# The last four experts as one group, and a scheduler that prices changes of array shape

## The chip, the cores and the metric

The kernel runs on one core of a Trainium2 chip. A core has TensorE (PE in the profile, its weight loads PEld), VectorE (DVE), ScalarE (ACT), GpSimd (POOL) and SyncE (SP), which here issues the DMAs. The metric is the device time of one execution in microseconds (us). A run's time is a little longer than the span of its trace, which goes from the first to the last instruction.

## The reference

Two transformer blocks over 256 tokens of width 1024, all in float32. The first has a modulated mixer (a spatial gating half, a convolution half) and a feed-forward part. The second has a pooling and a sparse attention mixer, an attention to a memory, and then a mixture of 32 experts, of which each token takes two of the eight in its group:

```python
g_sel = jnp.argmax(g_logits, axis=-1)
top_v, top_i = lax.top_k(e_in, TOP_K_EXPERTS)
top_w = jax.nn.softmax(top_v, axis=-1) * g_w
...
for g in range(N_GROUPS):
    a = jnp.einsum('nd,edf->nef', hf, w_gate[g])
    b = jnp.einsum('nd,edf->nef', hf, w_up[g])
    hid = jax.nn.silu(a) * b * gates[:, g, :, None]
    out = out + jnp.einsum('nef,efd->nd', hid, w_down[g])
return x + out
```

An expert has two matrices of 1024x256 (gate, up) and one of 256x1024 (down). All 32 make 96 loads of 1 MB, about half of the 212 MB that the kernel reads.

## The kernel before, in words

The weights lie in one stream in the order of `plan()` (line 217), in loads of 128 rows by 2048 numbers (1 MB). SBUF has 26 regions (`R0` to `R25`) of that size; most loads go to a region that has come free, in the stream's order, on SP's one queue. A DMA is issued when the region's last reader has run, and at most eight are under way.

`Recorder` records every operation with what it depends on, and `flush` (line 737) then orders them. `plan` (line 567) is a list scheduler: it steps through a time of its own in which an operation has the cost that `cost` (line 366) gives it, and picks on each engine the operation that can start first, by rank among those that can start together. `back` (line 700) makes new ranks from a finished order, and `PATH` (line 804) lists the rounds and the seeds of small changes to the ranks; the last order is issued. So each engine's instructions stand in one fixed order, and the engines wait for each other by semaphores. Nearly all instructions therefore have line 797, where `issue` emits them.

Where the scheduler sees TensorE idle for long enough, `plan` puts in products of a matrix of ones whose result nobody reads (`filler`, line 769, emitted at line 774). 92 such products stand in the order, 37 of them at the start.

Some matmuls use a part of the 128x128 array. A *column step* is four matmuls with 32 output rows each, side by side in four column tiles (`tile_position`), recorded as one operation (`rec.join`). `ada_pe` (line 1165) and `conv_pe` (line 1312) use them in the first block, the experts at lines 1939 to 1944 and 1969 to 1974. The value products of two attentions write 64 output rows, products of heads read 64 rows, and a few write or read 8.

`experts` (line 1914) goes over `GROUPS` (line 214): seven groups of four experts, and then two of two. The tokens of an expert stand in 32 slots. A group does this:

- `gather`: 16 products pick the tokens (`xg`).
- `gu`: eight column steps over the contraction (k), one load of 1 MB each, make gate and up in one bank `pg`. In a group of two a step has two column tiles, and one load holds two steps.
- `hid`: silu on ScalarE, a product on VectorE, two transposes.
- `dn`: four column steps with the down matrix make the experts' outputs `pd`, copied to `ye`. In a group of two, two experts and the two halves of the contraction take the four column tiles, and the halves are added in `combine` (`sw` is copied to both).
- `combine`: eight products by the weights `sw` add to the output `ac`.

The last group goes by quarters of 256 features in a fixed order (`rec.series`): `product`, `moved`, then `closing`, which combines, adds the residual and starts the output's DMA. A loop behind it takes tokens beyond 32 in an expert; in this input it doesn't run.

Of the kernel before, what the change touches and what calls it, by code (L numbers as in the profile page):

```python
# [15 lines left out]
KT = D // 128  # L16
# [78 lines left out]
def layout(v):  # L95
# [51 lines left out]
    for name, arg in PLAN:  # L147
# [17 lines left out]
        elif name == "fin":  # L165
            j = 256 * arg
            full(rowk(np.concatenate([fin[:, j:j + 256], fin[:, DF + j:DF + j + 256]], 1)))
        elif name == "fout":
            full(rowk(fout[512 * arg:512 * arg + 512]))
        elif name == "in2":  # L170
            pad = np.zeros((D, 56), np.float32)
            a = np.concatenate([win2[:, 2560:2632], pad, win2[:, 2048:2560], win2[:, 512:1536]],
                               1)[:, 512 * arg:512 * arg + 512]
            full(rowk(a) if arg == 0 else stat(a))
        elif name == "in2p":
            full(rowk(win2[:, 0:512]))
        elif name == "in2v":
            full(rowk(win2[:, 1536:2048]))
        elif name == "out2":
            full(rowk(wout2[512 * arg:512 * arg + 512]))  # L180
        elif name == "mk":
            full(rowk(wkv[:, 0:512]))
        elif name == "mv":
            full(rowk(wkv[:, 512:1024]))
        elif name == "wq":
            full(rowk(wq[:, 256 * arg:256 * arg + 256]))
        elif name == "wo":
            full(rowk(wo))
        elif name in ("gu", "dn"):
            (g_, s_), (q, e0, n) = arg, GROUPS[arg[0]]  # L190
            gg, e = q // 2, slice(4 * (q % 2) + e0, 4 * (q % 2) + e0 + n)
            if name == "gu":
                a = np.concatenate([eg[gg, e], eu[gg, e]], axis=-1).reshape(n, KT, 128, 512)
                full(a[:, 8 // n * s_:8 // n * (s_ + 1)].transpose(2, 1, 0, 3))
            elif n == 4:
                full(ed[gg, e].reshape(4, 2, 128, 2, 512)[:, s_].transpose(1, 2, 0, 3))
            else:
                full(ed[gg, e].reshape(2, 2, 128, 4, 256).transpose(2, 3, 1, 0, 4))
# [15 lines left out]
GROUPS = [(q, 0, 4) for q in range(7)] + [(7, 0, 2), (7, 2, 2)]  # L214


def plan():
# [13 lines left out]
    for g, (q, e0, n) in enumerate(GROUPS):  # L231
        p += [("gu", (g, s)) for s in range(n)] + [("dn", (g, s)) for s in range(n // 2)]
# [118 lines left out]
class Op:  # L351
    __slots__ = ("eng", "name", "args", "kw", "pos", "preds", "succs", "new", "bufs", "cost",
                 "set", "start", "end", "active", "calls")
# [12 lines left out]
def cost(eng, name, args, kw):  # L366
# [7 lines left out]
    if eng == "tensor":  # L374
# [4 lines left out]
        if "tile_position" in kw:  # L379
            return mv.free() * passes / 2.4e3 / 4 + 0.002  # L380
# [19 lines left out]
def activity(name, kw, c):  # L400
# [4 lines left out]
    return c if n >= 128 else c * n / 128  # L405

# [32 lines left out]
class Recorder:  # L439
# [3 lines left out]
    def __init__(self, nc, pools):  # L443
# [3 lines left out]
        self.hosts, self.series, self.joined = {}, None, None  # L447
# [39 lines left out]
    def record(self, eng, name, args, kw):  # L487
        if self.joined:
            op = self.joined[0]
            assert op.eng == eng  # L490
            c = cost(eng, name, args, kw)
# [16 lines left out]
        op.set = SETS.get(kw.get("func")) if eng == "scalar" else None  # L508
        self.ops.append(op)
# [57 lines left out]
    def plan(self, prio):  # L567
# [22 lines left out]
        table, oldest, order = None, 0, []  # L590
# [27 lines left out]
        while issued < n:  # L618
            best = None
            for e, rows in cands.items():  # L620
                pick = None
                for ready, op in rows:
# [10 lines left out]
                    rank = prio[op.pos] - (SWITCH if op.set and op.set != table else 0.0)  # L633
                    if pick is None or t < pick[0] or rank > pick[1]:
# [33 lines left out]
            if op.eng == "tensor":  # L668
                w = int(t / WINDOW)
# [131 lines left out]
SWITCH = 3.0  # L801
# [12 lines left out]
def _build(tc, a, out, ctx):  # L814
# [1093 lines left out]
    def combine(g, ye, sw, ac, ns=range(8)):  # L1908
        for j in ns:
            PE.matmul(out=ac[j], lhsT=ye[:, 128 * j:128 * j + 128], rhs=sw,  # L1910
                      start=(g == 0 and j % 2 == 0), stop=(g == len(GROUPS) - 1),
                      skip_group_check=True)

    def experts(ac, s8):
# [4 lines left out]
        for g, (q, e0, n) in enumerate(GROUPS):  # L1919
            if q % 2 == 0:  # L1920
                if s8 is None:
                    s8 = places(q)
                s8q, s8 = s8, None
                w8 = buf("U", 2, 8, CAP)
            if e0 == 0:
                gather(xg, s8q, q)
            if q % 2 == 0:
                for t in range(2):
                    V.tensor_tensor(out=w8[:, t], in0=s8q[:, t],
                                    in1=wt[:, t, 4 * q:4 * q + 8].unsqueeze(2).to_broadcast(  # L1930
                                        [128, 8, CAP]), op=ALU.mult)
            rows, first = slice(0, 32 * n), 4 * (q % 2) + e0
            pg = bank()
            k = 0
            for c in range(n):
                for reg in take("gu", (g, c), 2 if (g, c) == (len(GROUPS) - 1, 1) else 1):
                    w = view(reg, 0, 4 // n, n, 512)
                    for kk in range(4 // n):
                        with rec.join():
                            for e in range(n):  # L1940
                                o_ = 32 * (first + e)
                                PE.matmul(out=pg[32 * e:32 * e + 32], lhsT=xg[:, k, o_:o_ + 32],
                                          rhs=w[:, kk, e], start=(k == 0), stop=(k == KT - 1),
                                          tile_position=(0, 32 * e), skip_group_check=True)
                        k += 1
            S.activation(out=hid[rows], in_=pg[rows, 0:256], func=AF.Silu)
            V.tensor_tensor(out=hid[rows], in0=pg[rows, 256:512], in1=hid[rows], op=ALU.mult)
# [3 lines left out]
            for t in range(2):  # L1951
                PE.transpose(out=ps[rows, 128 * t:128 * t + 128],
                             in_=w8[:, t, first:first + n].rearrange("p e c -> p (e c)"),
                             identity=ident)
            for b in range(0, 128, 32 * n):
                S.copy(out=sw[b:b + 32 * n], in_=ps[rows, 0:T])
            ps = bank()
            for f in range(2):
                PE.transpose(out=ps[:, 128 * f:128 * f + 32 * n],
                             in_=hid[rows, 128 * f:128 * f + 128], identity=ident[rows, rows])  # L1960
            V.tensor_copy(out=hT.rearrange("p (f c) -> p f c", f=2)[:, :, rows],
                          in_=ps[:, 0:T].rearrange("p (f c) -> p f c", f=2)[:, :, rows])
            pd = [bank(), bank()]
            end = g == len(GROUPS) - 1
            if n == 4:
                for f in range(2):
                    for i, reg in enumerate(take("dn", (g, f))):
                        w = view(reg, 0, 4, 512)
                        with rec.join():
                            for e in range(4):  # L1970
                                PE.matmul(out=pd[i][32 * e:32 * e + 32],
                                          lhsT=hT[:, 128 * f + 32 * e:128 * f + 32 * e + 32],
                                          rhs=w[:, e], start=(f == 0), stop=(f == 1),
                                          tile_position=(0, 32 * e), skip_group_check=True)
# [4 lines left out]
            regs = take("dn", (g, 0), 2 if end else 1)  # L1979
            def product(i, m):  # L1980
                w = view(regs[i], 0, 2, 2, 2, T)
                with rec.join():
                    for f in range(2):
                        for e in range(2):
                            b = 64 * f + 32 * e
                            PE.matmul(out=pd[i][b:b + 32, T * m:T * m + T],
                                      lhsT=hT[:, 128 * f + 32 * e:128 * f + 32 * e + 32],
                                      rhs=w[:, m, f, e], start=True, stop=True,
                                      tile_position=(0, b), skip_group_check=True)

            def closing(i, m):
                j = 4 * i + 2 * m
                combine(g, ye, sw, ac, (j, j + 1))
                V.tensor_tensor(out=xt[:, j:j + 2], in0=ac.b[j // 2], in1=xt[:, j:j + 2],
                                op=ALU.add)
                SY.dma_start(out=out[:, j:j + 2], in_=xt[:, j:j + 2])

            def moved(i, m):
                c = 512 * i + T * m
                (V.tensor_copy if m else S.copy)(out=ye[:, c:c + T], in_=pd[i][:, T * m:T * m + T])  # L2000

            if end:
                steps = [(0, 0), (0, 1), (1, 0), (1, 1)]
                rec.series = {}
                for i, m in steps[:1]:
                    product(i, m)
                    moved(i, m)
                for n_, (i, m) in enumerate(steps):
                    if n_ + 1 < 4:
                        product(*steps[n_ + 1])  # L2010
                        moved(*steps[n_ + 1])
                    closing(i, m)
                rec.series = None
                continue
            for i in range(2):
                for m in range(2):
                    product(i, m)
            S.copy(out=ye[:, 0:512], in_=pd[0])
            V.tensor_copy(out=ye[:, 512:1024], in_=pd[1])
            last = (g, ye, sw, ac)  # L2020

# [4 lines left out]
    rounds = nc.values_load(nr.ap()[0:1, 0:1], min_val=1, max_val=8)  # L2026
    with tc.For_i(1, rounds, 1):
# [21 lines left out]
```

## Time and profile before

| | |
|---|---|
| median of three runs | 750.11 us (748.1 to 750.91) |
| profiled execution | 751.32 us, span 749.6 us |
| TensorE | 718.4 us busy (96%), 5466 records |
| VectorE, ScalarE | 418.1 us (56%), 311.3 us (42%) |
| stream's DMA queue | 211.55 MB, 72.9% of the 16 engines' time |
| granted TensorE clock | 0.987 on average |

A float32 product stands in the trace as two records. In rows of the timeline the third column from the engine is the operation with its tiles, then rows and columns of the array that it uses (128*32 is one column tile), then the output's shape; `xN` counts records, and what stands in brackets is idle time before it and what ended it. PE spans overlap a little, so that the start of the next row tells when an engine went on.

### The profile page before, as it was taken

How to read it: one execution, taken by the hardware profiler on the slowest of the kernel's cores; microseconds unless marked ns; L12 is line 12 of the kernel's file. 1: busy time of each engine (PE TensorE's matmuls, PEld its weight loads, DVE VectorE, ACT ScalarE, POOL GpSimd, SP SyncE). 2: the span in 40 equal slices, each digit the busy share in tenths (PEclk: the TensorE clock that was granted, in tenths of full speed). 3: DMA queues.
4: the chain of work that ended last, by engine and by line, in shares of the span. 5: the costliest groups of instructions: out<-in, count | busy, mean ns of one | idle time of the engine just before them, and what ended most of it. 6: DMA issues, size and time to landing. Idle time of an engine off the chain costs nothing.

```text
span 749.6 us, 13378 instructions
## 1 busy us (share of the span) xinstructions
PE 718.4 (96%) x5466; PEld 569.5 (76%) x5466; DVE 418.1 (56%) x876; ACT 311.3 (42%) x597; POOL 3.7 (0%) x18
## 2 busy tenths in 40 slices
PE   9999999999999999999999999999999999987894
PEld 9689676989999999999899768998844555442342
DVE  7679958694667577557787888466711221110002
ACT  6547647443544353446854547366521121110000
POOL 0010000000000000000000000000000000000000
PEclk9999999999999999999999999999999999999898
DMA  8997389996458668655621325973799999999981
GB/s 331 419 417 305 136 338 421 397 393 226 154 210 291 253 217 295 224 174 186 263 68 57 113 70 211 335 281 129 268 401 419 418 420 419 419 418 419 421 339 61
DMA packets 31603, 212.46 MB, mean 283 GB/s; under 512 B 3632, under 2 KB 4016, under 8 KB 7088
## 3 DMA queue, kind: packets, MB, share of 16 engines
q1 hardware_dynamic: 31536, 211.55, 72.9%
q8 instruction: 45, 0.74, 0.4%
q14 instruction: 22, 0.18, 0.1%
HBM read 210.48 MB, written 1.05 MB: 282 GB/s over the span
## 4 chain that ended last, share of the span: by engine, by line
PE 86%; DMA 7%; DVE 3%; ACT 1%; SPq 1%; issue 1%; ACTq 0%
PE B L797 85%; DMA R<-stream 7%; DVE R L797 2%; ACT R L797 1%; SPq L797 1%; PE B L774 1%; DVE s L797 0%; DVE U L797 0%; DVE gi L797 0%; DVE g L797 0%; DVE lgt L797 0%; DVE j L797 0%; DVE cond L797 0%; DVE i L797 0%; DVE ei L797 0%
## 5 line engine op out<-in xcount | busy, mean ns | idle before, releaser
L797 PE MATMUL B<-R,R 128*128 128x256 f32 (+4 forms) x4376 | 580.5, 366 | 12.3 <-DMA R<-stream 7.9
L797 PEld LDWEIGHTS B<-R,R 128*128 128x128 f32 (+2 forms) x4376 | 433.1, 169 | 86.7 <-issue 45.8
L797 ACT ACTIVATE R<-R 128x1024 fp32r<-128x1024 f32 (+4 forms) x268 | 187.9, 738 | 160.5 <-PE B L797 122.4
L797 DVE TENSOR_TENSOR R<-R,R 128x1024 fp32r<-128x1024 f32 (+3 forms) x214 | 192.0, 929 | 77.9 <-ACT R L797 73.8
L797 DVE TENSOR_TENSOR R<-B,R 128x256 f32<-128x256 f32 (+3 forms) x78 | 32.8, 440 | 72.3 <-ACT R L797 58.1
L797 ACT ACTIVATE R<-B 128x256 f32<-128x256 f32 (+4 forms) x82 | 27.6, 372 | 79.5 <-PE B L797 79.3
L797 ACT ACTIVATE R<-B,cv 128x128 f32<-128x128 f32 (+2 forms) x64 | 26.5, 423 | 79.3 <-PE B L797 79.0
L797 PEld LDWEIGHTS B<-U,R 128*128 128x128 f32 x256 | 34.0, 191 | 25.7 <-issue 19.3
L797 PE MATMUL B<-R 128*128 128x256 f32 (+4 forms) x200 | 49.0, 383 | 1.0 <-ACT R L797 1.0
L797 DVE COPY R<-B 128x256 f32<-128x256 f32 (+2 forms) x33 | 15.2, 464 | 59.1 <-PE B L797 59.0
L797 PEld LDWEIGHTS B<-R 128*128 128x128 f32 (+1 forms) x200 | 30.7, 193 | 21.0 <-issue 14.8
L797 ACT COPY R<-B 128x256 f32<-128x256 f32 (+3 forms) x35 | 13.9, 409 | 73.4 <-PE B L797 73.3
L797 DVE TENSOR_SCALAR R<-B,cv 128x128 f32<-128x128 f32 x32 | 11.2, 350 | 54.9 <-PE B L797 54.5
L797 PE MATMUL B<-U,R 128*128 128x128 f32 x256 | 40.2, 287 | 1.1 <-ACT R L797 0.7
L774 PEld LDWEIGHTS B<-ones 128*128 128x128 f32 x184 | 26.4, 217 | 13.9 <-issue 10.9
L774 PE MATMUL B<-ones 128*128 128x128 f32 x184 | 30.9, 313 | 1.5 <-POOL inv_h L797 1.4
L797 DVE SCALAR_TENSOR_TENSOR U<-R,ca,U 128x512 f32<-128x512 f32 x42 | 31.4, 748 | 0.6
L797 DVE SCALAR_TENSOR_TENSOR R<-R,cv,R 128x256 f32<-128x256 f32 (+1 forms) x54 | 25.2, 481 | 2.8 <-ACT R L797 1.7
L797 PE MATMUL B<-cst,R 128*128 128x128 f32 (+3 forms) x130 | 21.3, 255 | 4.3 <-DVE R L797 3.3
L797 PEld LDWEIGHTS B<-cst,R 128*128 128x128 f32 (+1 forms) x130 | 17.0, 163 | 8.7 <-DVE R L797 4.7
L797 ACT ACT_TABLE_LOAD x16 | 20.5, 1283 | 4.0 <-PE B L797 3.0
L797 DVE TENSOR_TENSOR R<-R 128x256 f32<-128x256 f32 x47 | 18.1, 421 | 2.1 <-ACT R L797 1.6
(123 smaller groups left out, 277.7 us busy)
## 6 DMA issues: line engine op xcount, KB each, us to landing
R<-stream SPq DMA_DIRECT2D x190, 1024.0 KB, 10.9
R<-stream SPq DMA_DIRECT2D x14, 512.0 KB, 12.0
R<-mt SPq DMA_DIRECT2D x2, 512.0 KB, 6.9
R<-xt SPq DMA_DIRECT2D x1, 1024.0 KB, 10.7
out_dram<-R SPq DMA_DIRECT2D x4, 256.0 KB, 2.5
cst<-cst SPq DMA_DIRECT2D x1, 533.0 KB, 18.7
R<-bands SPq DMA_DIRECT2D x1, 320.0 KB, 2.8
R<-cosin SPq DMA_DIRECT2D x1, 256.0 KB, 7.4
```

Source lines behind the costliest of these rows:

```text
L774: self.nc.tensor.matmul(out=self.pools["B"][k][:, 0:128], lhsT=ones, rhs=ones, start=True, stop=True)
L797: getattr(getattr(self.nc, op.eng), name)(*[real(v) for v in args], **{k: real(v) for k, v in kw.items()})
```

## The change

1. The last four experts are one group. `GROUPS` is 8, all groups have four experts, and each step four column tiles. In the last group the down matrix lies in the stream by quarters of the features, one load of 1 MB for each (the last two loads as two halves); a quarter is two column steps of 256 columns into a bank of its own, a copy to `ye`, two products of `combine`, the add and the output's DMA.
2. In the scheduler a column step of four costs what one of its matmuls costs (before, the sum of four quarters: nearly the same), a change of the array's shape costs time (`turn`), and an operation with another shape than the last loses half a microsecond of rank (`TURN`).
3. `PATH` is another list. No ones-matmul is put in behind the start of the experts (`rec.busy`).

```diff
-GROUPS = [(q, 0, 4) for q in range(7)] + [(7, 0, 2), (7, 2, 2)]
+GROUPS = 8
...
+def turn(a, b):
+
+    if not a or a == b:
+        return 0.0
+    c = 0.09 if b[0] < 128 or b[1] < 128 else 0.0
+    c += 0.188 if a[0] < 128 else 0.135 if a[1] < 128 else 0.0
...
+                    if op.shape and op.shape[0:2] != form[0:2]:
+                        rank -= TURN
...
-                room = t - lo
+                room = t - lo if op.pos < self.busy else 0.0
...
-PATH = (0, 4, 0, 31, 36, 0, 63, 0, 88, 120, 121, 144, 195, 343, 433, 447, 465, 779, 910)
+PATH = (0, 0, 11, 0, 63, 67, 74, 0, 89, 239)
...
+            regs = take("dn", (g, 0)) + take("dn", (g, 1), 2)
+
+            def quarter(c):
+                ps = bank()[:, 0:T]
+                for f in range(2):
+                    product(ps, view(regs[c], 1024 * f, 4, T), f)
+                (V.tensor_copy if c % 2 else S.copy)(out=ye[:, T * c:T * c + T], in_=ps)
+
+            rec.series = {}
+            quarter(0)
+            for c in range(4):
+                if c < 3:
+                    quarter(c + 1)
+                combine(g, ye, sw, ac, (2 * c, 2 * c + 1))
+                V.tensor_tensor(out=xt[:, 2 * c:2 * c + 2], in0=ac.b[c], in1=xt[:, 2 * c:2 * c + 2],
                                 op=ALU.add)
...
+    rec.busy = len(rec.ops)
     experts(Accum(), s8_0)
```

The order of TensorE changes nearly everywhere. Three places of it follow; in a row stand what is written, what is read, and its size, and names are bank or region, its version and a number.

TensorE in the second attention's mixer, where its value products (64 output rows) stand among those of the pooling input and transposes, before:

```order
L797 MATMUL B3_84<-R20_5_4497,R23_10_4131 64x128 x2
L797 MATMUL B4_85<-R24_6_4545,R4_5_3634 128x256
L797 MATMUL B4_85<-R10_6_4538,R4_5_3634 128x256
L797 MATMUL B6_87<-R10_6_4538,R2_4_3633 128x256
L797 MATMUL B3_84<-R18_8_4573,R23_10_4131 64x128 x4
L797 MATMUL B7_88<-cst_90,R20_5_4497 128x128
L797 MATMUL B1_82<-R20_5_4497,R23_10_4131 64x128 x2
```

The same place in the change:

```order
L823 MATMUL B0_81<-R0_4_4534,R18_4_3627 128x256
L823 MATMUL B5_86<-R22_9_4519,R5_5_3626 128x256
L823 MATMUL B0_81<-R22_9_4519,R18_4_3627 128x256
L823 MATMUL B5_86<-R0_4_4534,R5_5_3626 128x256
L823 MATMUL B3_84<-R24_4_4467,R13_5_4090 64x128 x2
L823 MATMUL B3_84<-R21_9_4555,R13_5_4090 64x128 x4
L823 MATMUL B6_87<-R24_4_4467,R13_5_4090 64x128 x2
```

Four of these pairs that stood in three places now stand together. Over the whole order up to the router, visits to a part of the array fall from 59 (40 to column tiles, 19 to 64 or 8 rows) to 40 (25 and 15).

TensorE between the first block's mixer and its feed-forward part, before: the last output products, the column sums of the modulation (`cst`, 128x4), the norm (`inv_d`, `ones`), the first feed-forward products:

```order
L797 MATMUL B2_83<-R21_2_1309,R11_0_165 128x256
L797 MATMUL B3_84<-cst_90,U1_62 128x4 x4
L774 MATMUL B6_87<-ones_91 128x128 x2
L797 MATMUL B4_85<-inv_d_92,R15_0_216 128x1 x4
L774 MATMUL B5_86<-ones_91 128x128 x3
L797 MATMUL B6_87<-R15_0_216,ones_91 128x128 x2
L774 MATMUL B1_82<-ones_91 128x128 x4
L797 MATMUL B5_86<-R11_1_1634,R14_3_1362 128x256
```

In the change:

```order
L823 MATMUL B0_81<-R2_2_1296,R12_0_166 128x256
L823 MATMUL B7_88<-R6_2_1249,R0_0_125 32x512 x4
L823 MATMUL B7_88<-R21_2_1264,R0_0_125 32x512 x4
L823 MATMUL B5_86<-inv_d_92,R15_0_216 128x1 x4
L823 MATMUL B3_84<-cst_90,U1_62 128x4 x4
L823 MATMUL B1_82<-R15_0_216,ones_91 128x128 x2
L800 MATMUL B6_87<-ones_91 128x128 x3
L823 MATMUL B4_85<-R10_1_1615,R23_4_1404 128x256
```

The last two of eight column steps of the modulation (loads `R6_2`, `R21_2`), which stood among the products of the mixer, now stand behind the last output product, and three ones-matmuls stand where nine stood.

TensorE at the end, before, from the last `gu` steps (`R9_5` holds the tokens) to the last `combine`:

```order
L797 MATMUL B3_84<-R3_13_6259,R9_5_5371 32x512 x2
L774 MATMUL B4_85<-ones_91 128x128 x2
L797 MATMUL B6_87<-cst_90,R1_9_5487 128x64 x2
L797 MATMUL B4_85<-R12_8_6270,R1_9_5487 32x256 x4
L774 MATMUL B2_83<-ones_91 128x128
L797 MATMUL B4_85<-R12_8_6270,R1_9_5487 32x256 x4
L797 MATMUL B5_86<-R1_9_5487 128x256 x2
```

In the change:

```order
L823 MATMUL B7_88<-R22_14_6184,R20_9_5363 32x512 x4
L823 MATMUL B7_88<-R1_12_6191,R20_9_5363 32x512 x4
L823 MATMUL B6_87<-cst_90,R12_7_5479 128x128 x2
L823 MATMUL B3_84<-R9_11_6198,R12_7_5479 32x256 x8
L823 MATMUL B0_81<-R7_6_6204,R12_7_5479 32x256 x8
L823 MATMUL B2_83<-R12_7_5479 128x256 x2
L823 MATMUL B7_88<-R10_6_6214,R12_7_5479 32x256 x8
```

One load of 1 MB is now one `gu` step of four tiles, not two steps of two; and a quarter of the down matrix (8 matmuls, two steps) reads one load. Visits to a part of the array behind the router fall from 70 to 47. On SP the order of the loads is as before up to the last group; 24 loads of the experts stand ahead of the read of the router's count in both.

## Rows read from the trace of the kernel before

**Rows 1.** The page's 40 slices of the span: clock and DMA, in tenths.
```profile
PEclk9999999999999999999999999999999999999898
DMA  8997389996458668655621325973799999999981
```

**Rows 2.** Busy time by stretch; the first row names the columns.
```profile
core 0: us, PE busy (x) PEld busy (x) DVE busy (x) ACT busy (x) POOL busy (x), PEclk, DMA share, GB/s
157.00:351.00 194.00, 194.00 (x1621) 193.98 (x1621) 126.19 (x177) 84.47 (x121) 0.00 (x0) 1.00 0.65 233
359.00:489.00 130.00, 130.00 (x894) 111.26 (x893) 99.36 (x239) 70.82 (x160) 0.00 (x0) 1.00 0.43 152
545.00:585.00 40.00, 40.00 (x336) 18.86 (x338) 7.87 (x21) 7.12 (x17) 0.00 (x0) 1.00 1.01 418
585.00:725.00 140.00, 126.86 (x832) 60.80 (x824) 18.55 (x45) 16.32 (x41) 0.00 (x0) 0.98 1.01 418
728.00:730.00 2.00, 2.00 (x10) 0.69 (x11) 0.00 (x0) 0.00 (x0) 0.00 (x0) 1.00 0.10 39
```

**Rows 3.** The chain that ended last, from 499 us: start, length, what.
```profile
539.71 98.69 PE B L797 x751
...
648.83 20.08 DMA R<-stream
...
676.45 19.89 DMA R<-stream
```

**Rows 4.** TensorE's timeline at two places of the second block.
```profile
640.25 2.78 PE L797 MATMUL B<-R,R 128*32 128x512 f32 x24 [0.52 <-DVE R L797]
...
645.02 1.07 PE L797 MATMUL B<-R,R 128*32 128x512 f32 x8
646.02 1.13 PE L797 MATMUL B<-R 128*128 128x256 f32 x4
646.99 0.38 PE L797 MATMUL B<-U,R 128*128 128x128 f32 x2
...
433.75 0.70 PE L797 MATMUL B<-R 64*128 64x256 f32 x4
434.38 0.49 PE L797 MATMUL B<-R,R 128*128 128x512 f32 x1
```

**Rows 5.** Timeline around the first feed-forward part: TensorE, VectorE, SP.
```profile
123.16 1.07 PE L797 MATMUL B<-R,R 128*32 128x512 f32 x8
148.92 0.95 PE L797 MATMUL B<-cst,U 128*128 128x4 f32 x8
156.91 1.27 PE L797 MATMUL B<-R,R 128*128 128x256 f32 x7
...
150.32 0.48 DVE L797 TENSOR_SCALAR U<-R,ca 128x512 f32<-128x512 f32 x1
153.03 0.75 DVE L797 SCALAR_TENSOR_TENSOR U<-R,ca,U 128x512 f32<-128x512 f32 x1
...
148.99 0.81 SPq L797 DMA_DIRECT2D R<-stream  x2
```

**Rows 6.** The page's group of table loads on ScalarE.
```profile
L797 ACT ACT_TABLE_LOAD x16 | 20.5, 1283 | 4.0 <-PE B L797 3.0
```

**Rows 7.** TensorE's timeline where it waits for loads, and stretches around the clock's fall.
```profile
678.92 1.07 PE L797 MATMUL B<-R,R 128*32 128x512 f32 x8 [0.56 <-DMA R<-stream]
679.91 0.71 PE L774 MATMUL B<-ones 128*128 128x128 f32 x4
681.42 1.07 PE L797 MATMUL B<-R,R 128*32 128x512 f32 x8 [0.79 <-DMA R<-stream]
...
696.38 1.93 PE L797 MATMUL B<-R,R 128*32 128x512 f32 x8 [1.43 <-DMA R<-stream]
...
693.00:696.40 3.40, 1.09 (x12) 0.18 (x12) 0.00 (x0) 0.00 (x0) 0.00 (x0) 1.00 1.01 419
696.40:703.30 6.90, 6.21 (x21) 1.99 (x22) 0.30 (x1) 0.58 (x1) 0.00 (x0) 0.51 1.01 420
```

**Rows 8.** The end: the last quarter's timeline.
```profile
738.16 0.64 PE L797 MATMUL B<-R,R 128*32 128x256 f32 x8
...
738.73 2.00 PE L797 MATMUL B<-R 128*128 128x256 f32 x8
...
740.76 0.69 DVE L797 TENSOR_TENSOR R<-B,R 128x512 f32<-128x512 f32 x1 [0.17 <-PE B L797]
```

More of the change, by code (lines that the diff above doesn't have):

```diff
@@ L352 @@
     __slots__ = ("eng", "name", "args", "kw", "pos", "preds", "succs", "new", "bufs", "cost",
-                 "set", "start", "end", "active", "calls")
+                 "set", "start", "end", "active", "calls",
+                 "shape")
 class Engine:
@@ L405, in activity, with shape @@
     return c if n >= 128 else c * n / 128
+def shape(op):
+    if op.name == "transpose":
+        return 128, 128, 1
+    rows, cols = op.kw["rhs"].shape[0], op.kw["out"].shape[0]
+    return rows, cols, 0 if any(s[0] == "bitcast" for s in op.kw["rhs"].steps) else 1
+def turn(a, b):
[3 more added lines that the diff above has]
+    c += 0.188 if a[0] < 128 else 0.135 if a[1] < 128 else 0.0
+    if not c and a[2] > b[2]:
+        return -0.083
+    return c if a[0:2] != b[0:2] else 0.0
 def latency(a, b):
@@ L490, in record @@
             assert op.eng == eng
-            c = cost(eng, name, args, kw)
+            c = 0.0 if "tile_position" in kw else cost(eng, name, args, kw)
             op.cost += c
@@ L589, in plan @@
         cands = {e: [] for e in ENGINES}
-        table, oldest, order = None, 0, []
+        table, oldest, order, form = None, 0, [], (128, 128, 0)
         cold, active = [True] * 4, {}
@@ L1928, in experts @@
                 for t in range(2):
                     V.tensor_tensor(out=w8[:, t], in0=s8q[:, t],
-                                    in1=wt[:, t, 4 * q:4 * q + 8].unsqueeze(2).to_broadcast(
+                                    in1=wt[:, t, 4 * g:4 * g + 8].unsqueeze(2).to_broadcast(
                                         [128, 8, CAP]), op=ALU.mult)
-            rows, first = slice(0, 32 * n), 4 * (q % 2) + e0
+            first, end = 4 * (g % 2), g == GROUPS - 1
             pg = bank()
@@ L1934, in experts @@
             k = 0
[L1935 to L1945, printed above, removed]
@@ L1946, in experts @@
-            S.activation(out=hid[rows], in_=pg[rows, 0:256], func=AF.Silu)
-            V.tensor_tensor(out=hid[rows], in0=pg[rows, 256:512], in1=hid[rows], op=ALU.mult)
+            for c in range(4):
+                for reg in take("gu", (g, c), 2 if end and c == 3 else 1):
+                    w = view(reg, 0, 4, 512)
+                    with rec.join():
+                        for e in range(4):
+                            o_ = 32 * (first + e)
+                            PE.matmul(out=pg[32 * e:32 * e + 32], lhsT=xg[:, k, o_:o_ + 32],
+                                      rhs=w[:, e], start=(k == 0), stop=(k == KT - 1),
+                                      tile_position=(0, 32 * e), skip_group_check=True)
+                    k += 1
@@ L1951, in experts @@
             for t in range(2):
-                PE.transpose(out=ps[rows, 128 * t:128 * t + 128],
-                             in_=w8[:, t, first:first + n].rearrange("p e c -> p (e c)"),
+                PE.transpose(out=ps[:, 128 * t:128 * t + 128],
+                             in_=w8[:, t, first:first + 4].rearrange("p e c -> p (e c)"),
                              identity=ident)
-            for b in range(0, 128, 32 * n):
-                S.copy(out=sw[b:b + 32 * n], in_=ps[rows, 0:T])
+            S.copy(out=sw, in_=ps[:, 0:T])
@@ L1957, in experts @@
             ps = bank()
             for f in range(2):
[L1959 to L1965, printed above, removed]
+                PE.transpose(out=ps[:, 128 * f:128 * f + 128], in_=hid[:, 128 * f:128 * f + 128],
+                             identity=ident)
@@ new lines, in experts, with product @@
+            V.tensor_copy(out=hT, in_=ps[:, 0:T])
+            def product(ps, w, f):
+                with rec.join():
+                    for e in range(4):
+                        PE.matmul(out=ps[32 * e:32 * e + 32],
+                                  lhsT=hT[:, 128 * f + 32 * e:128 * f + 32 * e + 32],
+                                  rhs=w[:, e], start=(f == 0), stop=(f == 1),
+                                  tile_position=(0, 32 * e), skip_group_check=True)
+            if not end:
+                pd = [bank(), bank()]
@@ L1966, in experts @@
                 for f in range(2):
                     for i, reg in enumerate(take("dn", (g, f))):
[L1968 to L1974, printed above, removed]
+                        product(pd[i], view(reg, 0, 4, 512), f)
@@ L1978, in experts @@
                 continue
[L1979 to L1994, printed above, removed]
-                                op=ALU.add)
[L1996 to L2014, printed above, removed]
```

51 lines of the change are left out of this document (27 added, 24 removed).

## The prediction

> **What bounds the kernel now.** I began with the page's slices [rows 1]: the clock and the DMA share in 40 pieces of 18.7 us. The reader is to see that the DMA engines are full from slice 29 on (543 us) and not steadily so before, and that the clock dips once, late. The table of stretches [rows 2] fills that in. TensorE is busy all of 157 to 351, 359 to 489 and 545 to 585 us: up to there it is the bound, whatever the loads do. From 585 to 725 it is busy for 126.86 of 140 us while the DMA stays at 418 GB/s: here the loads take over.
>
> Where they take over, the chain that ended last shows [rows 3]: PE alone from the router (539.71) for 98.69 us, to 638.40, and then long stretches of DMA. So the kernel has two bounds in a row. Up to the router, and some 100 us beyond it, TensorE; from about 640 us the stream. The stream's start is tied to the first part: its regions come free as the operations before the router run, and in both orders the same 24 loads of experts stand ahead of the read of the router's count. So if the router comes x us sooner, the stream ends x us sooner, with nothing else changed.
>
> The end is a third place. In 728 to 730 the DMA share is down to 0.10 [rows 2]: the last bytes have come, and I take 730.0 as the time at which TensorE could use them. But the last quarter's product starts at 738.16, and the last add ends at 740.76 + 0.69 = 741.45 [rows 8]. TensorE trails its loads by 8 us there, for it does groups 8 and 9 in steps of two column tiles, which cost as much as steps of four and carry half, and a part of them at the lower clock [rows 7]. Behind the add, up to the span's end at 749.6, only the output's DMA and the closing are left; the change leaves them alone.
>
> **The change part by part. First, visits to a part of the array.** Three column steps in a row take 2.78 us, one alone 1.07 [rows 4]: (2.78 - 1.07) / 2 = 0.855 each. A step alone puts the next start at 1.00 later (645.02 to 646.02), 0.145 more. Behind it the two 256-column products start their successor 0.97 later (646.02 to 646.99); they stream as many columns as a step, so 0.855 would do: 0.11 more. A visit to column tiles thus costs 0.145 + 0.11 = 0.25 us. Four value products on 64 output rows stream half of a step's columns, 0.43, and take 0.63 (433.75 to 434.38): 0.20 a visit. Up to the router 15 visits to column tiles and 4 to 64 or 8 rows go: 15 x 0.25 + 4 x 0.20 = **-4.6 us**. TensorE is the bound in most of that stretch, so I take all of it; the other end is zero, if the time comes back as waits for VectorE, which is busy 99.36 of 130 us in 359 to 489 [rows 2].
>
> **Second, the two column steps of the modulation** leave the full stretch around 123 us [rows 5] and stand behind the last output product, where TensorE had nothing but ones-matmuls between the column sums (from 148.92) and the feed-forward part (156.91). Each takes 1.00 out of the full stretch: -2.0, and I count -1.95. They bring work into the gap, 1.7 us, but replace six ones-matmuls, and what sets the gap is VectorE and ScalarE. What else moves with them: VectorE's operations on the modulation (0.48 at 150.32, 0.75 at 153.03), which stood among the norm's, now wait for the two steps and come behind it; of their 1.23 us I take 0.8 off the chain, between 0 and 1.23. The two loads' regions are held 25 us longer. On SP the load at that place waited for TensorE until 148.99 anyway, so I take nothing for it; if it were not covered, the stretch from 157 on has a DMA share of 0.65 and room for it. Sum **-2.75**, between 0 and -3.2.
>
> **Third, ScalarE's tables.** The order switches tables 19 times where it did 16, with a load of 1.283 us each [rows 6]. The three more stand in the first 100 us, where TensorE is fed by other work; of the 20.5 us of all sixteen only 4.0 stand behind a wait. I take 0; uncovered they cost 3 x 1.28 = +3.85.
>
> **Fourth, the ones-matmuls.** 28 of 92 stood behind the router; they go. Before the catch-up TensorE had none waiting there, after it they filled waits for loads [rows 7], so nothing is gained in time by that, and what it may cost is the clock (below).
>
> **Fifth, the last four experts as a group.** Behind the router the visits fall by 23, worth 23 x 0.25 = 5.8 us, and the steps of two by eight, worth 8 x 0.855 = 6.8 us. In the part that the stream paces neither counts by itself: it lets TensorE reach its loads sooner and stay with them. With steps of four, one load of 1 MB is one step. At 418 GB/s it comes every 2.5 us, and a step takes 1.07, with a transpose or combination here and there. So the trailing goes, and the last quarter starts when its load is there. From the start of the last quarter to the last add before took 741.45 - 738.16 = 3.29 us [rows 8]; the same pieces stand there after (two steps of 256 columns, a copy, two products, an add), so 730.0 + 0.1 + 3.3 = 733.4 against 741.45: -8.0. At the lower clock the last products (0.43 for the last step, four of 0.43 around it) would take 2.15 more; I give that one chance in three and take **-7.0**. Bounds: -8.0 from above, and from below -2.85 (the second rival).
>
> On the clock the trace shows this [rows 7]. While ones-matmuls filled the wait (678.92, 679.91, 681.42) a step took 1.07. In the 3.4 us before 696.40 TensorE was busy for 1.09 and the clock still 1.00; from there it was 0.51, 1.2 GHz, and a step took 1.93; it stayed so over 6.9 us in which TensorE was busy for 6.21, and then rose. The Trainium skill, in "TensorE: Matmul & The Clock Gate", section "HAM oscillation — how this bites in real kernels", describes a loop that waits for a load in each turn and starts each turn with a throttled clock, every time. The trace agrees for the one wait without ones-matmuls in it and shows no repeated one. By that rule the whole paced end would run at 1.2 GHz and the second rival would be the forecast.
>
> **Sum.** To the router -4.6 - 2.75 = -7.35; at the end -7.0; together -14.35. The profiled execution took 751.32: 751.32 - 14.35 = 736.97. It lies 1.21 above the median of the runs, 750.11, so **735.7 us**.
>
> **The rivals.** *Tail only.* The visits go but the time is given back: a chain over VectorE and ScalarE sets the second block, and the turns become waits. For it: VectorE's share in 359 to 489. Against it: TensorE has no wait in that stretch. 750.11 - 7.0 = 743.1.
>
> *Cold end.* Without ones-matmuls the clock falls once TensorE waits for every load. A step of 1.93 still goes into 2.5 us, so TensorE trails only where the gather, the transposes and the combinations add up; then it is busy, and the row says that the clock comes back. One such fall as in [rows 7] does 6.21 us of work at half speed, some 3 us too late, and at the end 2.15 more: 8.0 - 3.0 - 2.15 = 2.85 gained. 751.32 - 7.35 - 2.85 - 1.21 = 739.9. For it: nothing fills the waits any more. Against it: a lag from a fall earlier than the last group is made up.
>
> *No change.* The turns are given back and the three table loads are not covered: 743.1 + 3.85 = 747.0.
>
> *Slower: the clock falls when TensorE first meets a wait, and stays.* Behind the router TensorE's work before is 5.3 + 40.0 + 126.86 + 15.7 (to 740.73) = 188; less 5.8 and 6.8, 28 ones-matmuls of 0.36 (0.71 for two [rows 7]) and 3 for the cold stretch, 162 are left. The router is at 539.71 - 7.35 = 532.4. To end where it does now it may take 207 us. At half speed from x on it takes x + 2 (162 - x): it is slower if x is under 117, a fall before about 649 us. The catch-up is near x = 100 (98.69 before): 224 us, 17 too many, so 750 + 17 = 767. For it: no ones-matmul stands behind the router. Against it: the clock of [rows 7] came back as soon as TensorE was busy; and in 545 to 585 it is at 1.00 without any.
>
> **How the numbers follow.** Forecast (731 to 740) 0.58, tail only 0.17, cold end 0.14, no change 0.06, slower 0.05. The best case is -4.6 - 3.2 - 8.0 = -15.8 on 750.11, or 734.3; with the runs' own spread of 1 or 2 us below, and some waits that the better order may take out besides, 730. Above, tail only with a cold last quarter is 743.1 + 1 = 744, so the range is **730 to 745**. A measurement of this kernel tells about 0.5%, 3.75 us, from no change: 746.4 is the edge. Forecast, tail only and cold end lie below it: faster 0.88 (a little of "tail only" spills over), same 0.07, slower 0.05.
>
> **What would show it.** Visits: the router's products near 532 us and TensorE without a new wait in the second block. The moved steps: the first feed-forward product some 2.7 us plus the first block's share of the turns ahead of 156.91, and both steps inside the gap. Tables: 19 loads, with no more idle time in front of them than 4 us. Stream: full to about 722.5. End: the last add 3.3 to 5.5 us behind the last load, with DMA as what ends TensorE's waits in the whole of the last two groups. Clock: dips only from the catch-up on, each of a few us. I am wrong if the router is where it was, if TensorE is still behind its loads at the end, or if the clock stays at 1.2 GHz over a stretch in which TensorE is busy.

## The result and the profile after

The changed kernel takes 738.24 us (median of four runs, 737.02 to 738.67), the kernel before 750.06 in the same comparison: a ratio of 0.9843 (95% interval 0.9821 to 0.9866). A second comparison (experiment 1) gave 738.31 against 752.14, 0.981 (0.978 to 0.984). The forecast was 735.7 of 750.11, a ratio of 0.981, with a range of 730 to 745.

The page's slices of the profile after, which answer to [rows 1]:

```profile
PEclk9999999999999999999999999999899999987787
DMA  8997399599468876444811315973789999999993
```

Counted from 0, the stream is as full as before from slice 30 on. The clock now dips in more slices: once at slice 28, at the router, and in the last five. Falls of 3.4 us don't show in these tenths: the trace of the kernel before, where [rows 1] show one dip, has two more, at 153.72 and 355.11 us. The same stretches as in [rows 2] (us, then busy time of TensorE, its weight loads, VectorE, ScalarE, GpSimd, the granted clock, the DMA share, GB/s):

```profile
157.00:351.00 194.00, 193.30 (x1606) 192.46 (x1606) 128.03 (x177) 84.71 (x119) 0.00 (x0) 1.00 0.68 249
359.00:489.00 130.00, 128.67 (x929) 114.49 (x928) 102.42 (x249) 74.25 (x168) 0.00 (x0) 1.00 0.44 160
545.00:585.00 40.00, 39.54 (x322) 18.60 (x318) 7.48 (x19) 7.18 (x17) 0.00 (x0) 1.00 1.01 420
585.00:725.00 140.00, 121.60 (x798) 51.53 (x794) 19.52 (x46) 14.76 (x38) 0.00 (x0) 0.89 1.00 413
```

TensorE is still the bound up to the router; the time given back as waits in the second block is small (it is busy 128.67 of 130 us). In the last row the clock is 0.89 where it was 0.98. The chain that ended last shows where the bound changes hands; [rows 3] had 98.69 us of TensorE behind the router, here it is 20.46:

```profile
534.02 20.46 PE B L823 x172
554.50 18.90 DMA R<-stream
...
710.67 14.16 DMA R<-stream
724.88 3.49 PE B L823 x16
728.39 0.69 DVE R L823
```

So the loads are the end's chain from 554.50 to 724.88, and TensorE's last piece is short. The end, against [rows 8]: the last quarter waits for its load, which it did not before.

```profile
724.88 0.64 PE L823 MATMUL B<-R,R 128*32 128x256 f32 x8 [1.80 <-DMA R<-stream]
725.45 2.90 PE L823 MATMUL B<-R 128*128 128x256 f32 x8
...
728.39 0.69 DVE L823 TENSOR_TENSOR R<-B,R 128x512 f32<-128x512 f32 x1 [1.02 <-PE B L823]
```

The closing products take 2.90 where they took 2.00: they run at 1.2 GHz. The router, first as it was and then as it is; the rows are the norm, the logits' products of 40 columns, transposes, ones-matmuls and the first product that counts tokens:

```profile
532.62 1.03 PE L797 MATMUL B<-inv_d,R 128*128 128x1 f32 x8
533.51 0.84 PE L797 MATMUL B<-R,R 128*128 128x40 f32 x6
534.18 1.94 PE L797 MATMUL B<-cst,R 128*128 128x128 f32 x16
535.96 1.73 PE L774 MATMUL B<-ones 128*128 128x128 f32 x14
537.99 0.41 PE L797 MATMUL B<-asum,cst 128*128 128x32 f32 x2 [0.30 <-DVE asum L797]
```

```profile
524.43 0.36 PE L823 MATMUL B<-inv_d,R 128*128 128x1 f32 x2
...
526.91 3.65 PE L823 MATMUL B<-cst,R 128*128 128x128 f32 x16
530.36 2.20 PE L800 MATMUL B<-ones 128*128 128x128 f32 x12
532.40 0.31 PE L823 MATMUL B<-asum,cst 128*128 128x32 f32 x2
```

At the norm the change is ahead by 532.62 - 524.43 = 8.2 us, at the count by 537.99 - 532.40 = 5.6. In between the sixteen transposes take 3.65 us for 1.94: the granted clock was 0.50 from 525.00 to 531.83. Places that are the same in both orders, before, after, and the change once more (experiment 1), in us:

| place | before | after | again |
|---|---|---|---|
| first feed-forward product | 156.91 | 151.35 | 152.49 |
| first 512-column product, second block | 352.38 | 348.05 | 349.73 |
| pooling products | 424.67 | 419.38 | 419.53 |
| the norm some 40 us ahead of the router | 498.11 | 489.57 | 489.70 |
| count of tokens (router) | 537.99 | 532.40 | 530.02 |
| end of the last add | 741.45 | 729.08 | 725.24 |

### The profile page after: what moved, and what is told of

The parts are those of the page before. It is cut to its first block, busy times and chain, and to the rows that moved or that the text cites. A ratio compares the mean times of both kernels' runs of the same rounds, so it can differ in the third digit from the quotient of the medians.

```text
span 737.0 us, 13178 instructions
## 1 busy us (share of the span) xinstructions
PE 703.4 (95%) x5374; PEld 560.9 (76%) x5374; DVE 415.0 (56%) x873; ACT 314.0 (43%) x595; POOL 3.0 (0%) x18
## 4 chain that ended last, share of the span: by engine, by line
PE 69%; DMA 25%; DVE 2%; ACT 2%; issue 1%; SPq 1%; ACTq 0%
PE B L823 69%; DMA R<-stream 25%; ACT R L823 2%; DVE R L823 1%; SPq L823 1%; DVE s L823 0%; PE B L800 0%; ACT s L823 0%; DVE U L823 0%; DVE pos L823 0%; ACTq L823 0%
## 5 line engine op out<-in xcount | busy, mean ns | idle before, releaser
L823 DVE TENSOR_TENSOR R<-B,R 128x256 f32<-128x256 f32 (+2 forms) x77 | 32.3, 439 | 77.8 <-ACT R L823 55.1
L823 ACT ACTIVATE R<-B 128x256 f32<-128x256 f32 (+3 forms) x81 | 27.0, 370 | 83.4 <-PE B L823 83.3
L823 PE MATMUL B<-R 128*128 128x256 f32 (+4 forms) x184 | 46.6, 387 | 1.5 <-ACT R L823 1.5
L823 ACT COPY R<-B 128x256 f32<-128x256 f32 (+2 forms) x31 | 12.3, 407 | 69.5 <-PE B L823 69.4
L823 DVE TENSOR_SCALAR R<-B,cv 128x128 f32<-128x128 f32 x32 | 11.2, 350 | 50.3 <-PE B L823 49.8
L823 PE MATMUL B<-U,R 128*128 128x128 f32 x256 | 38.4, 285 | 0.9 <-ACT R L823 0.5
L823 PE MATMUL B<-cst,R 128*128 128x128 f32 (+2 forms) x128 | 22.3, 272 | 4.1 <-DVE R L823 3.0
L823 PEld LDWEIGHTS B<-cst,R 128*128 128x128 f32 x128 | 18.6, 176 | 7.9 <-DVE R L823 4.5
L800 PE MATMUL B<-ones 128*128 128x128 f32 x112 | 17.5, 321 | 1.4 <-POOL inv_h L823 1.4
L800 PEld LDWEIGHTS B<-ones 128*128 128x128 f32 x112 | 16.9, 236 | 1.4 <-POOL inv_h L823 1.4
```

What stands on the lines that cost most here:

```text
L800: self.nc.tensor.matmul(out=self.pools["B"][k][:, 0:128], lhsT=ones, rhs=ones, start=True, stop=True)
L823: getattr(getattr(self.nc, op.eng), name)(*[real(v) for v in args], **{k: real(v) for k, v in kw.items()})
```

## The experiments

In all experiments but 1 and 5 each engine is held to a written order, so that only what is named differs. The lines that do this:

```diff
+                    if op.pos in fixed and op.pos != heads[e][at[e]]:
+                        continue
```

**1. The change once more.** The same kernel.

> The changed kernel once more. In its first profile the clock was at 1.2 GHz from 525.00 to 531.83, just ahead of the router, and the router's products came 2.6 us later than the lead of 8.2 us at 516 to 524 would have had them. Theory A (the fall belongs to this order): the same fall again, the router's lead again 5.6 us, 738.2 us. Theory B (an accident of one profile): no fall there, the router's lead 8.2 us, and a time near 735.7.

738.31 us, ratio 0.981 (0.978 to 0.984); its six runs lie at 734.5 and 734.9, and at 738.0 to 738.8. The profiled one took 734.86:

```profile
526.13 1.94 PE L823 MATMUL B<-cst,R 128*128 128x128 f32 x16
527.91 1.50 PE L800 MATMUL B<-ones 128*128 128x128 f32 x12
530.02 0.41 PE L823 MATMUL B<-asum,cst 128*128 128x32 f32 x2 [0.61 <-DVE asum L823]
...
721.95 0.64 PE L823 MATMUL B<-R,R 128*32 128x256 f32 x8 [0.20 <-DMA R<-stream]
722.52 1.99 PE L823 MATMUL B<-R 128*128 128x256 f32 x8
```

The same program, transposes at 1.94, the router 8.0 ahead of before, the closing at 1.99. Theory A falls: the fall at the router isn't in every execution of the order. Over all thirteen traces of this study it stands in five: the change's first, experiments 6 and 7 in the order of the change, 2 and 5 in that of before. The two traces of the change differ by 3.8 us: 2.4 at the router, 0.9 in the closing products, 0.5 in the wait for the last loads. That the same falls make the two groups of times isn't shown, for the other executions have no trace; a run of 738.17 us in the first comparison has a mean clock of 0.980, the profiled 734.86 one of 0.979. Four of the six runs are in the later group, so that B is right on the trace (734.86) and not on the median.

**2. The tail alone.** The experts' code of the change, every engine in the order of before up to the last four experts, ones-matmuls kept. Against the kernel before:

```diff
-GROUPS = [(q, 0, 4) for q in range(7)] + [(7, 0, 2), (7, 2, 2)]
+GROUPS = 8
```

> Every engine in the order of before up to the last four experts, ones-matmuls as before, and only the last four experts as one group with its quarters. Theory A: the end by itself is worth what the sum had, -7.0, or -8.0 with the clock kept up: 742 to 743, with the router where it was and the last add some 3.4 us behind the last load. Rival: TensorE needs the turns saved behind the router as well to come level with its loads, so only half of it, 746.

746.01 us, ratio 0.9919 (0.989 to 0.9947): -6.1. In the trace the router is at 539.06 (with the fall, 1.1 later than before) and the last add ends at 734.66: 195.6 us from one to the other, where before took 741.45 - 537.99 = 203.5. That is 7.9 less, as the forecast's 7.0 to 8.0 had it. TensorE waits for its loads to the last group, and the clock holds, with the ones-matmuls in the waits:

```profile
726.20 1.07 PE L809 MATMUL B<-R,R 128*32 128x256 f32 x16 [0.55 <-DMA R<-stream]
...
731.94 1.99 PE L809 MATMUL B<-R 128*128 128x256 f32 x8
```

**3. The order alone.** The scheduler and the order of the change, two groups of two at the end, no ones-matmuls behind the router. Against the change:

```diff
-GROUPS = 8
+GROUPS = [(q, 0, 4) for q in range(7)] + [(7, 0, 2), (7, 2, 2)]
```

> The order of the change on every engine up to the last four experts, no ones-matmuls behind the router, but the last four experts as two groups of two as before. Theory A: the lead of the router alone, -5.2 to -5.6: 744.7; with the clock falling in the steps of two at the end up to 3 more: 748. Rival (the visits' time is given back as waits): 750.

740.92 us, ratio 0.9849 (0.9821 to 0.9878): -11.2, far more than either theory gave. The router is at 533.27, 4.7 ahead of before, and from there to the last add it takes 198.4 us, 5.1 less than before, with the old tail. Alone, the two parts make 11.2 + 6.1 = 17.3 us, together 13.8. So a piece of some 3.5 us is in both; behind the router the traces have 5.1 + 7.9 = 13.0 for the parts and 6.8 to 8.2 for both. What the piece is, experiments 5 and 9 asked.

**5. Before once more.** The same kernel.

> The kernel before once more. In the trace that the prediction was made from, the clock fell from 696.44 to 703.26 while TensorE worked behind its loads, and router to last add took 203.5 us; with the order of the change and the same two groups of two it took 198.4 (the run with the order alone). Theory A (of the 8 us by which TensorE trailed, about 3 were that fall): a profile without a fall there has 200 us from the router's first product to the last add; one with a fall there 203. Rival (the fall doesn't matter, the steps of two and the visits make all of the lag): 203.5 whatever the clock did.

750.01 us, ratio 0.9989 (0.9952 to 1.0027). In the trace the clock was at 1.2 GHz from 696.60 to 706.84, much as in [rows 7], and router to last add took 204.3. Both theories allow that; it tells nothing apart, except that the fall there is no accident of one trace.

**9. Before without the 28 ones-matmuls behind the router.**

```diff
-                room = t - lo
+                room = t - lo if op.pos < self.busy else 0.0
```

> The kernel before, every engine in its own order, only without the 28 ones-matmuls behind the router. In its trace they take 5.3 us of TensorE between 690 and 742, where TensorE trailed its loads. Theory A (there they delay the end one for one, so that most of the 7 to 8 us at the end was them and not the steps of two): router to last add 198 to 199 us in place of 203.5 and 204.3, the kernel 5 us faster, 745 to 746. Rival (the saved visits and the steps of four made the gain; without ones-matmuls the clock falls more): 203 us, no change.

748.47 us, ratio 0.9966 (0.9937 to 0.9995): -2.8 (0.4 to 4.7). Router (537.27) to last add (737.19): 199.9, that is 3.5 less than in [rows 8]'s trace. Theory A has the sign, and its size was too large. The row that it rested on, of the kernel before from 690 to 742 us:

```profile
L774 PE MATMUL B<-ones 128*128 128x128 f32 x26 | 5.3, 311 | 0.0
```

Thirteen products, 5.3 us, no idle time in front of them. That alone doesn't say that they delay anything, for the instruction behind them may have to wait anyway. The chain that ended last, in the kernel before, tells which do; its pieces of ones-matmuls are:

```profile
709.78 0.64 PE B L774 x4
712.26 0.64 PE B L774 x4
727.88 0.42 PE B L774 x2
729.28 0.42 PE B L774 x2
730.68 0.42 PE B L774 x2
```

Seven of the thirteen, 2.5 us, lie in the chain; the other six stand ahead of short waits for VectorE and ScalarE. Over the two stretches that hold the seven, at full clock in both traces, the kernel before took 11.13 us (704.54 to 715.67) and 7.90 (725.11 to 733.01), this one 9.97 and 6.27: 2.8 us less, as much as the time says. The other 0.7 of the 3.5 is what remains of falls of the clock in other places: before from 696.44 to 703.26, among work, where it took 13.6 us (690.92 to 704.54) for 10.0 here; here from 685.52 to 695.76, among waits, and from 729.89 to 733.30, where it took 10.0 us to the last add for 8.4 before.

So TensorE trails its loads in the kernel before, and there ones-matmuls in its queue delay the end. This piece was in both parts: experiment 3 had taken it away with the ones-matmuls, experiment 2 by letting TensorE keep up, so that most of them stand in waits. 11.2 - 2.8 = 8.4 is then left for the order, and 8.4 + 6.1 = 14.5 stands beside 13.8 for both; each of these is known to about 2 us. By the traces behind the router the piece is some 5 us; that the rest of it is the visits saved there, which also let TensorE keep up, is argued and not shown.

**8. The change with ones-matmuls behind the router.**

```diff
-                room = t - lo if op.pos < self.busy else 0.0
+                room = t - lo
```

> The changed kernel with ones-matmuls in the waits behind the router as well, placed by the same rule as ahead of it. Theory A (the clock falls in the paced end for want of them, but only the last fall costs time): no fall behind the router, router to last add 195.2 to 195.6 us in every execution where the change had 195.2 and 196.7, 737.5. Rival (they delay the steps that the loads release): 196.5 or more, 739.

737.29 us, ratio 0.9813 (0.9786 to 0.984), beside 0.981 of experiment 1: no difference that can be told. Router to last add took 195.5. The clock still fell twice behind the router, for 3.4 us each, where the change had 31 us of it (658 to 713) in one trace and 20 in the other. So A's saying that no fall would be left is wrong. Nor do the falls cost anything that can be told while the loads pace: 195.2 us with 20 us of them, 195.5 with 6.8.

**6. The two column steps back among the first mixer's products**, on TensorE alone.

```diff
 R,ones (2 products)
+column step of the modulation, one on either side
...
 last output product
-two column steps of the modulation
```

> The changed kernel with the two column steps of the modulation put back among the products of the first mixer, each by itself, on TensorE alone; the other engines' orders stay. Theory A (the steps filled a gap that something else sets): each costs its 1.0 us there and the gap stays as long: the stretch from the eight-row products to the first feed-forward product is 2.0 longer, 740.3. Rival (the gap is now TensorE's own work, with only 0.3 us of waiting in it): the gap shrinks by what the steps took there, and the sum is 0.3 to 0.5 longer, 738.7.

739.96 us, ratio 0.9846 (0.9817 to 0.9875). From the eight-row products (113.08) to the first feed-forward product (155.72) it took 42.64 us; in the change's traces with an equally long fall of the clock there (experiments 4 and 7) 40.25 and 40.27. So 2.4 longer, and the gap shows why:

```profile
149.45 0.83 PE L811 MATMUL B<-ones 128*128 128x128 f32 x6
151.37 1.17 PE L834 MATMUL B<-inv_d,R 128*128 128x1 f32 x8 [1.08 <-DVE R L834]
...
155.72 4.46 PE L834 MATMUL B<-R,R 128*128 128x256 f32 x23 [0.92 <-ACT R L834]
```

From the last product to the norm TensorE again has ones-matmuls and a wait for VectorE, where the two steps had stood; from the norm on, the gap is as long as it was (4.35; 4.31 in the change). Theory A, a little above its size. The time alone, 739.96 beside 738.31 in another comparison, would not tell it.

**7. Twelve value products set apart**, two full products between each and the next: 12 visits to 64 columns for 4.

```diff
-64 columns x4, 128 columns ..., 64 columns x5, ...
+64 columns, 128 columns x2, 64 columns, 128 columns x2, ...
```

> The changed kernel with the twelve value products on 64 output rows of the second mixer set apart, two full products between each and the next, on TensorE alone: 12 visits in place of 4, all else the same. Theory A (the price from the rows of before, 0.20 for such a visit): the stretch from the pooling products to the router's norm is 8 x 0.20 = 1.6 longer, 739.9. Rival (a visit of one product costs more than one of four, 0.33, as the 3.26 us that this stretch lost would have it): 2.6 longer, 740.9.

741.05 us, ratio 0.9852 (0.982 to 0.9884). From the pooling products to the next norm, with the clock at full speed in both; the change first, then this kernel:

```profile
419.38 0.38 PE L823 MATMUL B<-cst,s 128*8 128x128 f32 x2
489.57 0.50 PE L823 MATMUL B<-inv_d,R 128*128 128x1 f32 x4
```

```profile
421.32 0.38 PE L834 MATMUL B<-cst,s 128*8 128x128 f32 x2
494.26 0.50 PE L834 MATMUL B<-inv_d,R 128*128 128x1 f32 x4
```

70.19 and 72.94: 2.75 us for 8 visits, 0.34 each. The rival's price, not the 0.20 from [rows 4]: the row there, `64*128`, is of products that read 64 rows, and I took it for the value products, which stand as `128*64`.

**4, 10, 11. Four ones-matmuls among the router's products of 40 columns; four among the eight-row and two-column products at 113 us; both.**

```diff
+                if self.first and op.pos in WARM:
+                    order.append((WARM[op.pos], k[1]))
```

> The changed kernel with four products of the matrix of ones (0.85 us of TensorE) put singly among the router's sixteen products of 40 columns, nothing else. Theory A (the fall comes from the narrow products there, and costs 2.6): no fall ahead of the router, its lead 7.3 to 7.5 us, 736.4 us. Rival (the fall comes from something else): the fall stays and the time is 0.85 longer, 739.1.

> The changed kernel with four ones-matmuls (0.85 us) put singly among the four products that read eight rows and the four with two columns (112.7 to 115.8 in its profile), behind which the clock was at 1.2 GHz for 3.4 to 6.8 us in all traces but the first of before. Theory A (these narrow products bring the fall): no fall between 112 and 123, the stretch from there to the first feed-forward product 0.9 to 2.5 us shorter, 736.5. Rival (it falls all the same): 739.1.

> The changed kernel with four ones-matmuls among the eight-row and two-column products and four among the router's products of 40 columns. Theory A (both falls go): the router's first product at 528 to 529 plus the 1.7 that they take, so 530 in every execution, 736.5 and less spread than the 4 us of the change. Rival: 739 to 740.

737.85 us (0.9813, 0.9783 to 0.9843), 741.14 (0.985, 0.9813 to 0.9887) and 742.45 (0.9871, 0.983 to 0.9912). Experiment 4's trace has no fall at the router, but neither have those of 1, 3 and 8, without them; its time doesn't tell. In experiment 10 the clock fell all the same, from 114.52 to 124.76, longer than in any other trace at that place, and in experiment 11 from 116.89 to 123.71. Experiment 10:

```profile
113.45 0.49 PE L813 MATMUL B<-ones 128*128 128x128 f32 x2
113.87 1.47 PE L836 MATMUL B<-R,cst 8*128 8x256 f32 x4
115.27 0.80 PE L813 MATMUL B<-ones 128*128 128x128 f32 x2
```

So a few full products among the narrow ones don't keep the fall off at 113 us; whether the narrow ones bring it isn't shown. Experiments 10 and 11 are 3 and 4 us above the change, more than the 0.85 and 1.7 that they add; the trace of 10 has 20.5 us of falls ahead of the router, that of experiment 1 6.8. What decides in which execution the clock falls, and for how long, stays open.

## Why the prediction was right

The ratio of the second comparison is the forecast's, that of the first lies 0.3% above. The mechanism held: fewer visits and the moved steps bring the router forward, steps of four let TensorE keep up with its loads. That the sum came out so closely is in part luck: the parts ahead of the router were too small, and falls of the clock that it didn't have gave some of that back. Point by point:

- **Visits, -4.6: right in kind, wrong in their prices.** The 15 visits that I priced as column tiles are 6 to column tiles and 9 to 64 columns. From the pooling products to the norm the change gained 73.44 - 70.19 = 3.25 us, where 7 visits to columns and 3 to rows went; by 0.25 and 0.20 that would have been 2.35. Experiment 7 has 0.34 for a visit of one product to 64 columns. In the first block only executions with an equally long fall of the clock at 113 to 122 us can be compared. From the norm near 21 us to the end of the last output product experiment 5 (order of before) took 151.32 - 20.93 = 130.39 us, experiment 6 (the change with the two steps put back) 149.45 - 20.91 = 128.54: 1.85 us for seven visits fewer, 0.26 each, which is the forecast's price. That makes 5.1 us for 17 of the 19 visits.
- **The moved steps, -2.75: right in kind, too small.** Experiment 6 has 2.4 for TensorE's part, where I had 1.95. The time from the norm to the first feed-forward product went from 156.91 - 151.19 = 5.7 to 4.3, 1.4 where I had taken 0.8 for VectorE's part. The 3.8 together lie outside my bound of 3.2.
- **What I did not see there:** the clock falls behind this gap in every trace, before from 153.72 to 157.13. In that trace the fall lay in the gap; in the change's first it is from 149.53 to 152.94 and the feed-forward part starts at 151.35, inside it. That part takes 348.05 - 151.35 = 196.70 us for 195.47 before: 1.2 us of the lead given back. By estimate 0.8 of it is the fall (1.6 us at half the clock), and a wait for ScalarE ahead of 348.05 is 0.36.
- **Tables, 0: right.** 19 loads, and the idle time in front of them is 2.9 us (3.9 in experiment 1) for 4.0 in [rows 6]:

```profile
L823 ACT ACT_TABLE_LOAD x19 | 24.4, 1283 | 2.9 <-PE B L823 1.8
```

- **The router, -7.35: right in kind, a little small.** -8.2 at the norm; -8.0 at the count without the fall of the clock there, -5.6 with it. The trace before had no such fall, so a comparison of these two traces alone would have put 2.4 us on the change that aren't its own. Nor had it one at 113 to 122 us, where both traces of the change have 3.4 us of it. Experiments 2 and 1, with 3.4 us each there, took 532.50 - 20.96 = 511.54 and 524.57 - 21.59 = 502.98 us from the norm near 21 us to the router's norm: 8.6 for 7.35.
- **Ones-matmuls, "nothing is gained in time by that": the step that failed.** I looked at them where TensorE waits, in [rows 7], and not behind 700 us, where it trails. There they cost time; experiment 9 has 2.8 us of the kernel's (0.4 to 4.7). The sum came out because the -7.0 was counted from the last landing, and so held them already. In the change, where TensorE keeps up, it makes no difference that can be told whether they are there (experiment 8).
- **The end, -7.0: right.** 195.2 to 196.7 us from router to last add, for 203.5: -6.8 in the change's first trace and -8.2 in the second; 0.9 of the difference is the clock in the last quarter (2.90 and 1.99), which the one chance in three had at 2.15. That the steps of two made the trailing is only a part: without ones-matmuls and with the order of the change (experiment 3) the same steps end 2 to 3 us later than steps of four, 198.4 for 196.7 and 195.2, and not 8.
- **Rivals.** Tail only: no, experiment 3. Cold end: the falls are there, 31 us of them in the first trace, and a step of 1.94 still goes into 2.5. The Trainium skill's rule ("TensorE: Matmul & The Clock Gate", section "HAM oscillation — how this bites in real kernels") holds for this stretch in part: the clock falls again and again while TensorE waits for loads, not in every turn (31 of the 55 us from 658 to 713). TensorE's waits in that stretch are at most 1.4 us. Slower: no; each fall ended but the last, which began at 726.38, 2 us ahead of TensorE's last product.
- **Signs.** One that I had named as against me came: from 525.00 to 531.83 the clock stood at 1.2 GHz while TensorE was busy throughout. And dips came ahead of the catch-up too (115, 149, 351 and 525 us in the first trace). So what I had of the clock was wrong there, at a cost of a few us that the sum didn't have.

## What to carry to other kernels

A filler that is to keep the clock up belongs only where the engine waits; look at each place whether the engine is ahead of its loads or behind them, for behind them the filler delays the end. Idle time in front of the filler doesn't tell this, the chain that ended last does. Two parts of a change that cure the same lag don't add: take the piece that both hold out of the sum before forecasting each. And a fall of the clock that stands in one execution and not in the next is part of neither kernel: compare stretch by stretch with the clock's rows beside it, and look at a second trace before a difference of 2 us is explained.

## What was not expected of the hardware

With the same instructions in the same order the clock fell ahead of the router in one execution and not in another, after 16 us in which TensorE was busy throughout; it cost 2.4 us. Of thirteen full 128x128 products that were put into the end as fillers, 5.3 us of TensorE, seven lay in the chain that ended last and delayed it by 2.5 us. And a visit of a single product to 64 columns costs 0.34 us, more than the 0.25 of a visit to four column tiles.
